# One block of a hybrid transformer on one core: the joint down stage with two block sums made by adding loads, an eighth pair by seven products, and pairs interleaved

## The chip, the cores and the metric

The kernel runs on one core of a Trainium2 chip. The metric is the time of one execution on the device, in microseconds (us); of several runs the median is taken. A core has TensorE (PE; its weight loads are listed as PEld), VectorE (DVE), ScalarE (ACT), GpSimd (POOL), SyncE (SP) and 16 DMA engines. Here SP issues the weight loads and POOL a second stream of loads.

## The reference

One transformer block over 256 tokens of width 2048: adaptive normalisation, one wide projection, a gated recurrence (HGRN2) in both directions, windowed attention with rotary positions, a gated merge, and a convolutional feed-forward network. The part that the change touches is the last product:

```python
def conv_ffn(h, w_up, conv_w, conv_b, w_down):
    a, u = jnp.split(h @ w_up, 2, axis=-1)
    return (jax.nn.silu(depthwise_conv(a, conv_w, conv_b)) * u) @ w_down
...
new_x = x_mid + mod_x[:, 5][:, None, :] * ffn_x
```

`w_down` is 5632 x 2048, that is 44 row blocks of 128. Everything is float32.

## The kernel before

Work runs as one stream of weights. A float32 product is made of three products of TensorE (`mm3`): both operands are split into a high part (float32r, a cast on ACT) and a low part (the rest, a subtraction on DVE), and high x high, high x low and low x high are added in PSUM. So each 512 KB of weights costs a load by SP into a buffer `raw`, a cast into `whi` on ACT and a subtraction into `wlo` on DVE, and PE reads both. There are four buffers `raw`, three `whi` and three `wlo`: a new block's cast waits until PE is done with the block three before it.

The feed-forward network is worked off in three groups of 16, 16 and 12 row blocks. `up(0)` and `up(1)` make the activations `g0` and `g1` of the first 32 row blocks; then the joint down stage (`down_two`) multiplies all 32 with `w_down`; then the third group follows. The joint stage has two halves of 1024 output columns each (`half`). Within a half the 32 row blocks are 16 pairs; a pair of row blocks, two groups of 128 tokens and two halves of 512 columns make a product of 2 x 2 by 2 x 2 blocks. Of a pair's weights, W11 and W12 are the two column halves of its first row block, W21 and W22 those of its second. A plain pair takes eight block products, that is 24 instructions on PE. The pairs in `SEVEN` take seven block products (Winograd's form of Strassen's scheme), 21 instructions: three go into `sev`, and four banks `norm` collect the rest. The seven products need four sums of weight blocks, T1 to T4, each split into high and low parts as well: `two` (L990) makes T1 (W11 and W12) and T3 (W12 and W22) in a tile `araw` with two additions of 128x512 on DVE (L991, L992; the signs are in the activations), `four` (L997) makes the other two from it (L998, L999). They need sums of activations too, which `seven_acts` makes in `up(0)` and `up(1)` for each pair in `SEVEN`.

`chunk` (L137) issues a block's load, cast and subtraction with a priority that is up to `LEAD` = 60 steps ahead, so that a scheduler puts them ahead of the products that stand before them in the program. Each engine then runs its queue strictly in that order; a waiting instruction holds all behind it. In the profile L143 is the cast in `chunk` and L144 the subtraction, L148 the load, L69 every product. L112 to L114 are the same three in the other stages. At the end of a half the seven-product banks are combined on DVE and ACT (L1005 to L1013), and `turn` transposes the result on PE (L1022) and adds it to the residual `xm` (L1025). The second half takes over the PSUM banks of the first.

## Time and profile before

| | |
|---|---|
| median of 3 runs | 1676.38 us (1675.18 to 1677.02) |
| profiled execution | 1675.59 us, of which 1673.8 us are the span from the first to the last instruction |
| joint down stage | from about 1296 to 1469 us of the span |
| PE busy | 1660.3 us, 99% of the span |
| DVE busy | 1264.6 us, 76% |
| ACT busy | 862.1 us, 52% |
| granted TensorE clock | 1.0 in every stretch |

The page lists busy times of engines, groups of equal instructions by source line, DMA queues, and the chain of waits that ended last. Starts and durations of single instructions are read from the timeline. A product of 128x512 shows a duration of 0.39 us, but the next one starts after about 0.23 us, since products are pipelined: PE's pace is read from starts, and a wait is a start that comes later than that.

### The profile page before, as it was taken

What the parts mean: (1) busy time and instruction counts of PE and PEld (TensorE: products, weight loads), DVE (VectorE), ACT (ScalarE), POOL (GpSimd) and SP (SyncE); (2) the same over time, 40 slices, a digit from 0 to 9 for tenths busy, and PEclk for the clock granted to TensorE, in tenths of its full rate; (3) what the DMA queues carried; (4) which work ended last, traced back from release to release, by engine and by line L of the source; (5) the groups of instructions that cost most, each with busy time, mean ns of one, the idle gap of its engine ahead of it and who ended that gap; (6) DMA issues with size and microseconds to landing.
All of it is one profiled execution on the core that took longest, in us unless ns stands there. A gap on an engine that the chain in (4) does not pass through costs nothing.

```text
span 1673.8 us, 25069 instructions
## 1 busy us (share of the span) xinstructions
PE 1660.3 (99%) x9508; PEld 1392.2 (83%) x9508; DVE 1264.6 (76%) x2014; ACT 862.1 (52%) x1323; POOL 68.3 (4%) x132
## 2 busy tenths in 40 slices
PE   8999999999999999999999999999999999999999
PEld 3668888888888888888888988888888777788887
DVE  3448985666879886878879887788767888866665
ACT  4337542433646764554455665555555555545542
POOL 0000100000000000001100000000000000000000
PEclk9999999999999999999999999999999999999999
DMA  9997834534466657878856577677555565655554
GB/s 378 408 356 246 286 122 158 178 111 154 162 216 211 214 202 277 285 242 280 285 202 234 182 247 256 212 273 252 191 183 190 185 212 187 201 183 192 187 199 149
DMA packets 104153, 371.85 MB, mean 222 GB/s; under 512 B 11488, under 2 KB 13920, under 8 KB 104032
## 3 DMA queue, kind: packets, MB, share of 16 engines
q1 hardware_dynamic: 85600, 303.14, 51.3%
q0 software_dynamic: 18432, 67.12, 12.3%
q8 instruction: 74, 1.21, 0.3%
q14 instruction: 47, 0.39, 0.1%
HBM read 368.11 MB, written 2.10 MB: 221 GB/s over the span
## 4 chain that ended last, share of the span: by engine, by line
PE 96%; DMA 2%; DVE 1%; ACT 0%; issue 0%; SPq 0%; DVEq 0%; ACTq 0%
PE bankm L69 85%; PE banks L69 9%; DMA ringv<-in_wst_dram 1%; DMA ringq<-in_wst_dram 1%; PE banks L406 0%; PE banks L610 0%; PE banks L779 0%; PE banks L602 0%; DVE wlo L114 0%; DMA xraw<-in_xct_dram 0%; PE banks L611 0%; PE banks L224 0%; PE banks L632 0%; PE banks L749 0%; PE banks L1022 0%
## 5 line engine op out<-in xcount | busy, mean ns | idle before, releaser
L69 PE MATMUL bankm<-hl,whi 128*128 128x512 f32 (+1 forms) x3136 | 970.4, 392 | 0.0
L114 DVE TENSOR_TENSOR wlo<-raw,whi 128x1024 fp32r<-128x1024 f32 (+2 forms) x434 | 528.1, 1218 | 240.0 <-ACT whi L113 238.2
L113 ACT CAST whi<-raw 128x1024 fp32r<-128x1024 f32 (+2 forms) x434 | 453.2, 1045 | 479.5 <-PE bankm L69 366.4
L69 PEld LDWEIGHTS bankm<-hl,wlo 128*128 128x128 f32 x2848 | 533.2, 188 | 120.6 <-DVE wlo L114 0.4
L69 PE MATMUL bankm<-hl,wlo 128*128 128x256 f32 (+2 forms) x2848 | 610.2, 287 | 0.0
L69 PEld LDWEIGHTS bankm<-hl,whi 128*128 128x128 f32 x3136 | 494.9, 189 | 20.3 <-DVE hl L153 0.4
L69 PE MATMUL bankm<-whi,hl 128*128 128x512 f32 x640 | 209.2, 395 | 1.2 <-ACT hl L245 1.0
L398 DVE SCALAR_TENSOR_TENSOR acc<-araw,csil,acc 128x1024 f32<-128x1024 f32 x120 | 153.4, 1279 | 2.1 <-DMA araw<-in_ada_dram 1.6
L69 PEld LDWEIGHTS bankm<-whi,hl 128*128 128x128 f32 x640 | 119.7, 188 | 28.0 <-ACT hl L245 2.6
L69 PE MATMUL bankm<-wlo,hl 128*128 128x512 f32 x320 | 124.7, 392 | 0.0
L393 POOL DMA_DIRECT2D araw<-in_ada_dram x128 | 68.1, 532 | 1092.2 <-DVE acc L398 566.9
L143 ACT CAST whi<-raw 128x1024 fp32r<-128x1024 f32 x64 | 61.1, 956 | 42.1 <-PE bankm L69 25.4
L69 PE MATMUL bankm<-yb,whi 128*128 128x512 f32 x256 | 80.7, 397 | 0.0
L144 DVE TENSOR_TENSOR wlo<-raw,whi 128x1024 fp32r<-128x1024 f32 x64 | 69.3, 1104 | 2.2 <-ACT whi L143 1.1
L69 PEld LDWEIGHTS bankm<-wlo,hl 128*128 128x128 f32 x320 | 60.1, 188 | 12.9 <-DVE wlo L144 0.4
L69 PEld LDWEIGHTS bankm<-yb,wlo 128*128 128x128 f32 x256 | 48.1, 188 | 11.3
L910 ACT ACTIVATE fs<-fs,prm 128x256 f32<-128x256 f32 x44 | 26.4, 601 | 49.8 <-DVE fs L464 49.8
L69 PE MATMUL bankm<-yb,wlo 128*128 128x256 f32 x256 | 50.6, 279 | 0.0
L143 ACT CAST whi<-araw 128x1024 fp32r<-128x1024 f32 x28 | 29.5, 1054 | 34.3 <-PE banks L69 17.0
L144 DVE TENSOR_TENSOR wlo<-araw,whi 128x1024 fp32r<-128x1024 f32 x28 | 34.3, 1224 | 16.2 <-ACT whi L143 14.5
L69 PE MATMUL bankm<-whi,g 128*128 128x512 f32 x136 | 46.1, 390 | 0.0
L226 DVE TENSOR_REDUCE tn<-banks 128x8 f32<-128x32 f32 (+1 forms) x9 | 1.7, 188 | 53.1 <-ACT whi L113 50.1
(281 smaller groups left out, 1538.9 us busy)
## 6 DMA issues: line engine op xcount, KB each, us to landing
raw<-in_wst_dram SPq DMA_DIRECT2D x489, 512.0 KB, 4.1
araw<-in_ada_dram POOLq DMA_DIRECT2D x128, 512.0 KB, 4.7
ringv<-in_wst_dram SPq DMA_DIRECT2D x24, 512.0 KB, 9.9
ringq<-in_wst_dram SPq DMA_DIRECT2D x20, 512.0 KB, 9.9
araw<-in_wst_dram SPq DMA_DIRECT2D x10, 512.0 KB, 9.9
xraw<-in_xct_dram SPq DMA_DIRECT2D x8, 512.0 KB, 7.3
raw<-in_wst_dram SPq DMA_DIRECT2D x7, 384.0 KB, 9.9
ringkT<-in_wst_dram SPq DMA_DIRECT2D x5, 512.0 KB, 9.9
```

What stands on the lines that cost most here:

```text
L69: return PE.matmul(o, l, r, start=start, stop=stop, skip_group_check=True)
L113: S.copy(hi, raw)
L114: self.last = V.tensor_tensor(lo, raw, hi.bitcast(F32), op=ALU.subtract)
L143: S.copy(hi[:, w], raw[:, w])
L144: V.tensor_tensor(lo[:, w], raw[:, w], hi[:, w].bitcast(F32), op=ALU.subtract)
L226: V.tensor_reduce(m8, aps[:, 0:w].rearrange("p (q g c) -> p q c g", q=2 * n, g=4)[:, :, 0:2, :], axis=AX.X, op=ALU.add)
L393: nc.gpsimd.dma_start(raw, ada2[idx])
L398: V.scalar_tensor_tensor(acc, raw, csil[:, kt, 0:1], acc, op0=ALU.mult, op1=ALU.add)
L910: S.activation(t, s, AF.Identity, bias=cb[:, f:f + 1], scale=cw[:, f, 1:2])
```

## The change

In the joint down stage:

- T1 and T3 of a pair of `SEVEN` are no longer made on DVE. `ahead` loads the pair's first row block into `araw` by SP, and then a load by POOL adds W12 and W22 (in rows of 512 elements) to the tile's two halves while it writes (`accum_op=ALU.add`). This second load waits for the first. It is placed up to 2 x `LEAD` steps ahead.
- W11 is loaded a second time, alone (256 KB), and its high and low parts have a tile of their own (`w1`, in the place `kT`, one buffer) instead of a `whi` and a `wlo`. `four`'s sums go to `t24`, in the place `acc`, one buffer.
- Pair 15 joins `SEVEN`; pair 14 is the last plain pair and closes the sums. Pairs 1 to 12 are interleaved: between the parts of a seven-product pair stand the two halves of the next plain pair. Pairs 13 and 15 follow without one.
- `turn` of the first half stands after one of the two blocks of pair 0 instead of after both; the combination of the banks comes after pair 15.
- POOL's scratch for descriptors is 4096 instead of 8192.

```diff
-SEVEN = (1, 3, 5, 7, 9, 11, 13)
+SEVEN = (1, 3, 5, 7, 9, 11, 13, 15)
...
-    def chunk(parts, make, tag="raw"):
+    def chunk(parts, make, raw=None):
         with tc.high_priority(offset=min(LEAD, max(0, tc.tile_snap_priority() - base[0]))):
-            raw = strm.tile([P, 1024], F32, name=tag, bufs=4 if tag == "raw" else 2)
-            hi, lo = [strm.tile([P, 1024], F32R, name=nm, bufs=3) for nm in ("whi", "wlo")]
-            make(raw)
+            if raw is None:
+                raw = strm.tile([P, 1024], F32, name="raw", bufs=4)
+            elif raw is big:
+                raw = big.tile([P, 1024], F32, name="t24", tag="acc")
             w = slice(0, 512 * parts)
+            if parts == 2:
+                hi, lo = [strm.tile([P, 1024], F32R, name=nm, bufs=3) for nm in ("whi", "wlo")]
+            else:
+                one = big.tile([P, 2, 512], F32R, name="w1", tag="kT")
+                hi, lo = one[:, 0, :], one[:, 1, :]
+            if make:
+                make(raw)
...
+        def ahead(p):
+            with tc.high_priority(offset=min(2 * LEAD, max(0, tc.tile_snap_priority() - base[0]))):
+                r = strm.tile([P, 1024], F32, name="araw", bufs=2)
+                nc.sync.dma_start(r, wst[at(p, 0)])
+                nc.gpsimd.dma_start(r.rearrange("p (k c) -> p k c", k=2),
+                                    wst[at(p, 0):at(p, 0) + 2, :, 512:].rearrange("k p c -> p k c"), accum_op=ALU.add)
+            return r
+
+        def normal(p, k, start=False):
+            a = acts(p)[2 * k:2 * k + 2]
+            _, ws = chunk(2, block(p, k))
+            for b, (x, w) in zip((0, 2, 1, 3), ((x, w) for w in ws for x in a)):
+                add(norm[b], x, w, start)
+
+        def seven(p, between=lambda k: None):
+            r2 = ahead(p)
...
+            rb, (w21, w22) = chunk(2, block(p, 1))
             add(norm[0], a12, w21)
             add(norm[1], s4, w22)
-            ra, (w11,) = chunk(1, fetch)
+            between(1)
+            _, (w11,) = chunk(1, block(p, 0, 512))
             add(sev[0], a11, w11, f, l)
-
-            def two(raw):
-                V.tensor_tensor(raw[:, 0:512], ra[:, 0:512], ra[:, 512:], op=ALU.add)
-                V.tensor_tensor(raw[:, 512:], ra[:, 512:], rb[:, 512:], op=ALU.add)
-            r2, (t1, t3) = chunk(2, two, "araw")
+            _, (t1, t3) = chunk(2, None, r2)
             add(sev[1], s1, t1, f, l)
             add(sev[3], a21, t3, f, l)
+            between(0)
...
-            r4, (t2, t4) = chunk(2, four, "araw")
+            _, (t2, t4) = chunk(2, four, big)
...
+        normal(0, 1, True)
+        before()
+        normal(0, 0)
+        for p in range(1, 13, 2):
+            seven(p, lambda k: normal(p + 1, k))
+        seven(13)
+        seven(15)
...
-    nc = bacc.Bacc("TRN2", target_bir_lowering=False, num_devices=1, dynamic_dma_scratch_size=8192)
+    nc = bacc.Bacc("TRN2", target_bir_lowering=False, num_devices=1, dynamic_dma_scratch_size=4096)
```

What the scheduler makes of it. First DVE's queue in the middle of the first half, over one seven-product pair and one plain pair, before (`raw_12428` is the pair's W21 and W22, `raw_12440` its W11 and W12, `araw_12449` holds T1 and T3, `araw_12462` T2 and T4, the last two rows are the plain pair):

```order
L144 TENSOR_TENSOR wlo_12430<-raw_12428,whi_12429 128x1024
L991 TENSOR_TENSOR araw_12449<-raw_12440 128x512
L992 TENSOR_TENSOR araw_12449<-raw_12440,raw_12428 128x512
L144 TENSOR_TENSOR wlo_12442<-raw_12440,whi_12441 128x512
L998 TENSOR_TENSOR araw_12462<-araw_12449,raw_12428 128x512
L999 TENSOR_TENSOR araw_12462<-araw_12462,raw_12428 128x512
L144 TENSOR_TENSOR wlo_12451<-araw_12449,whi_12450 128x1024
L144 TENSOR_TENSOR wlo_12464<-araw_12462,whi_12463 128x1024
L144 TENSOR_TENSOR wlo_12477<-raw_12475,whi_12476 128x1024
L144 TENSOR_TENSOR wlo_12495<-raw_12493,whi_12494 128x1024
```

And after (`w1_12630` is W11, `araw_12596` T1 and T3, `raw_12599` W21 and W22, `t24_12665` T2 and T4, `raw_12611` and `raw_12647` the plain pair):

```order
L152 TENSOR_TENSOR w1_12630<-raw_12629,w1_12630 128x512
L1001 TENSOR_TENSOR t24_12665<-araw_12596,raw_12599 128x512
L152 TENSOR_TENSOR wlo_12601<-raw_12599,whi_12600 128x1024
L1002 TENSOR_TENSOR t24_12665<-t24_12665,raw_12599 128x512
L152 TENSOR_TENSOR wlo_12613<-raw_12611,whi_12612 128x1024
L152 TENSOR_TENSOR wlo_12638<-araw_12596,whi_12637 128x1024
L152 TENSOR_TENSOR wlo_12649<-raw_12647,whi_12648 128x1024
L152 TENSOR_TENSOR wlo_12667<-t24_12665,whi_12666 128x1024
```

The two additions L991 and L992 are gone, and the first addition that reads the added tile (L1001) stands ahead of the subtraction of W21 and W22.

Second, DVE's queue at the end of the first half. Before, pair 13 (`raw_12677`, `raw_12689`) is followed by the plain pairs 14 and 15 and the first combinations of banks:

```order
L998 TENSOR_TENSOR araw_12711<-araw_12698,raw_12677 128x512
L999 TENSOR_TENSOR araw_12711<-araw_12711,raw_12677 128x512
L144 TENSOR_TENSOR wlo_12700<-araw_12698,whi_12699 128x1024
L144 TENSOR_TENSOR wlo_12713<-araw_12711,whi_12712 128x1024
L144 TENSOR_TENSOR wlo_12731<-raw_12729,whi_12730 128x1024
L1006 TENSOR_TENSOR yva_12142<-banks_12139,ykT_12141 128x512
L144 TENSOR_TENSOR wlo_12749<-raw_12747,whi_12748 128x1024
L144 TENSOR_TENSOR wlo_12767<-raw_12765,whi_12766 128x1024
```

After, from pair 13's T1 and T3 (`araw_12678`) through pair 15 (`araw_12724`) to pair 14 (`raw_12777`, `raw_12783`) and the next half's first block (`raw_12825`):

```order
L152 TENSOR_TENSOR wlo_12702<-araw_12678,whi_12701 128x1024
L152 TENSOR_TENSOR wlo_12713<-t24_12711,whi_12712 128x1024
L1001 TENSOR_TENSOR t24_12757<-araw_12724,raw_12727 128x512
L152 TENSOR_TENSOR wlo_12729<-raw_12727,whi_12728 128x1024
L152 TENSOR_TENSOR w1_12740<-raw_12739,w1_12740 128x512
L152 TENSOR_TENSOR wlo_12748<-araw_12724,whi_12747 128x1024
L1002 TENSOR_TENSOR t24_12757<-t24_12757,raw_12727 128x512
L152 TENSOR_TENSOR wlo_12759<-t24_12757,whi_12758 128x1024
L152 TENSOR_TENSOR wlo_12779<-raw_12777,whi_12778 128x1024
L152 TENSOR_TENSOR wlo_12785<-raw_12783,whi_12784 128x1024
L152 TENSOR_TENSOR wlo_12827<-raw_12825,whi_12826 128x1024
```

Two seven-product pairs now stand without a plain pair between them, and pair 15's L1001 stands ahead of three subtractions of that pair.

Third, SP's queue at the same place. Before, four loads of 512 KB to each two pairs:

```order
L148 DMA raw_12677<-in_wst_dram 128x1024
L148 DMA raw_12689<-in_wst_dram 128x1024
L148 DMA raw_12729<-in_wst_dram 128x1024
L148 DMA raw_12747<-in_wst_dram 128x1024
L148 DMA raw_12765<-in_wst_dram 128x1024
```

After (L972 is the load that POOL's adding load then waits for):

```order
L972 DMA araw_12678<-in_wst_dram 128x1024
L964 DMA raw_12647<-in_wst_dram 128x1024
L964 DMA raw_12681<-in_wst_dram 128x1024
L964 DMA raw_12693<-in_wst_dram 128x512
L964 DMA raw_12727<-in_wst_dram 128x1024
L972 DMA araw_12724<-in_wst_dram 128x1024
L964 DMA raw_12739<-in_wst_dram 128x512
```

A seven-product pair has three loads on SP instead of two, besides the adding load on POOL, and there are two buffers `araw`.

More of the change, by code (lines that the diff above doesn't have):

```diff
@@ L145, in chunk @@
         return raw, [(hi[:, 512 * i:512 * i + 512], lo[:, 512 * i:512 * i + 512]) for i in range(parts)]
-    def fetch(raw):
-        nc.sync.dma_start(raw, wst[st.half])
-        st.half += 1
     def split(hi, lo, src):
@@ L931, in seven_acts @@
             sums["a"] = big.tile([P, 5, 2, 3 * P], F32R, name="sa", tag="v")
-            sums["b"] = big.tile([P, 2, 2, 3 * P], F32R, name="sb", tag="sb")
+            sums["b"] = big.tile([P, 3, 2, 3 * P], F32R, name="sb", tag="sb")
         n = SEVEN.index(p)
@@ new lines, in acts, with block, at @@
+        def acts(p):
+            return act(2 * p, 0), act(2 * p, 1), act(2 * p + 1, 0), act(2 * p + 1, 1)
+        def block(p, k, c=1024):
+            return lambda raw: nc.sync.dma_start(raw[:, 0:c], wst[at(p, k), :, 0:c])
+        def at(p, k):
+            return st.half + 32 * n + 2 * p + k
+        def ahead(p):
[5 more added lines that the diff above has]
+            return r
@@ L1028, in down_two @@
     def down_two(g0, g1):
-        ys = lambda: [big.tile([P, 2, 512], F32, name="y" + t, tag=t) for t in ("kT", "va")]
         sev = [bank()]
@@ L1036, in down_two @@
         sev = [bank() for _ in range(4)]
-        y1 = []
-        half(1, g0, g1, norm, sev, y1, lambda: (turn(0, y0, sev), y1.extend(ys())))
+        half(1, g0, g1, norm, sev, y1, lambda: turn(0, y0, sev))
         turn(1, y1, None)
+        st.half += 64
     def down(g, gt, last):
```

54 lines of the change are left out of this document (18 added, 36 removed).

## The prediction

> **What bounds the kernel now.** I read the page first, then the joint down stage by stretches, its waits, and the timelines of PE, ACT and DVE in it.
>
> ```profile
> span 1673.8 us, 25069 instructions
> PE 1660.3 (99%) x9508; PEld 1392.2 (83%) x9508; DVE 1264.6 (76%) x2014; ACT 862.1 (52%) x1323; POOL 68.3 (4%) x132
> PE 96%; DMA 2%; DVE 1%; ACT 0%; issue 0%; SPq 0%; DVEq 0%; ACTq 0%
> ```
>
> PE is the chain that ended last (96%). So a change is worth the products it takes from PE plus the waits of PE that it ends, less those it makes. Now the stage (columns: stretch, length, PE, PEld, DVE, ACT, POOL busy, clock, DMA share, GB/s), one plain and one seven-product pair long:
>
> ```profile
> 1306.40:1316.90 10.50, 10.50 (x47) 8.36 (x46) 9.16 (x12) 5.79 (x6) 0.00 (x0) 1.00 0.62 200
> ```
>
> DVE is busy for 9.16 of 10.50 us, close behind PE. The clock is full. PE's pace and its one wait, from PE's timeline of such a stretch:
>
> ```profile
> 1339.07 0.62 PE L69 MATMUL bankm<-whi,g 128*128 128x512 f32 x2
> ...
> 1343.17 0.62 PE L69 MATMUL bankm<-whi,g 128*128 128x512 f32 x2
> ...
> 1345.67 0.39 PE L69 MATMUL banks<-whi,g 128*128 128x512 f32 x1
> 1346.01 0.50 PE L69 MATMUL banks<-wlo,sa 128*128 128x512 f32 x1
> 1346.35 0.40 PE L69 MATMUL banks<-whi,sa 128*128 128x512 f32 x1
> ```
>
> Between the first two rows lie 18 products: 4.10 / 18 = 0.228 us each. The last three rows are 0.34 us apart instead: 0.22 us lost where T1 and T3 (`sa`) come in. The waits of the stage (1280 to 1480) say how often:
>
> ```profile
> PEld banks L69 <- DVE wlo L144: 2.6, 7, 0.4
> PEld bankm L69 <- DVE wlo L144: 2.6, 7, 0.4
> ```
>
> Seven in each half, one for each seven-product pair: 14 x 0.22 = 3.1 us. Their cause, on ACT and DVE:
>
> ```profile
> 1343.64 1.05 ACT L143 CAST whi<-araw 128x1024 fp32r<-128x1024 f32 x1 [2.14 <-PE bankm L69]
> ```
> ```profile
> 1340.93 0.69 DVE L992 TENSOR_TENSOR araw<-raw 128x512 f32<-128x512 f32 x1
> 1341.54 0.69 DVE L144 TENSOR_TENSOR wlo<-raw,whi 128x512 fp32r<-128x512 f32 x1
> 1342.15 0.69 DVE L998 TENSOR_TENSOR araw<-araw,raw 128x512 f32<-128x512 f32 x1
> 1342.87 0.69 DVE L999 TENSOR_TENSOR araw<-araw,raw 128x512 f32<-128x512 f32 x1
> 1344.73 2.59 DVE L144 TENSOR_TENSOR wlo<-araw,whi 128x1024 fp32r<-128x1024 f32 x2 [1.17 <-ACT whi L143]
> ```
>
> The sums are ready at 1343.56, but the cast waits for a buffer: PE's last product from the block three before starts at 1343.17, the cast at 1343.64 (0.47 later), the subtraction at 1344.73, the low part is used at 1346.01. Such a turn of a buffer takes 2.84 us from last product to first use; 12 dense products (2.74 us) lie between. W11's half block stands in that rotation and is only three products long, which makes the cover short. The other wait is at the boundary of the halves:
>
> ```profile
> 1390.30 0.70 PE L69 MATMUL bankm<-whi,sa 128*128 128x512 f32 x2
> 1390.84 0.39 PE L69 MATMUL banks<-whi,hl 128*128 128x512 f32 x1
> 1391.46 0.50 PE L69 MATMUL bankm<-whi,hl 128*128 128x512 f32 x1 [0.23 <-ACT whi L143]
> 1391.79 0.39 PE L69 MATMUL banks<-whi,hl 128*128 128x512 f32 x1
> ```
>
> 1391.79 - 1390.30 = 1.49 us for four products, 0.58 too long. In all 3.1 + 0.6 = 3.7 us.
>
> **The change, part by part.**
>
> *Products.* Pair 15 takes 21 instead of 24 in each half: 6 x 0.228 = 1.37 us less, on the path. Its extra sums of activations on DVE in `up(1)` cost nothing: the subtractions there stand idle for ACT, which waits for PE,
>
> ```profile
> 1283.01 1.23 DVE L114 TENSOR_TENSOR wlo<-raw,whi 128x1024 fp32r<-128x1024 f32 x1 [1.23 <-ACT whi L113]
> 1285.85 1.23 DVE L114 TENSOR_TENSOR wlo<-raw,whi 128x1024 fp32r<-128x1024 f32 x1 [1.61 <-ACT whi L113]
> ```
>
> and they are first needed half a stage later.
>
> *W11 out of the rotation.* The tightest turn is then that of the plain pair's first block: it waits for the previous plain block, and between lie T2 and T4 (6 products), W21 and W22 (6) and its own first: 14 starts = 3.19 us against 2.84. It holds, so the 3.1 us go, in pairs 1 to 12. Were the pace of DVE in the way, they would stay: the ends are 0 and 3.1. But L991 and L992 (685 ns, below) leave DVE, 9.16 - 1.37 = 7.79 us of a stretch of 45 x 0.228 = 10.26. I take 3.1. `w1` and `t24` with one buffer each turn over once in 10.26 us and cost nothing: `w1`'s products end 4.8 us after a pair's start, the next `w1` is read at 14.4. At the start of the stage `w1` takes the place `kT` from `up(1)`,
>
> ```profile
> 1301.68 0.42 DVE L915 TENSOR_TENSOR fs<-fs,fs 128x256 f32<-128x256 f32 x1
> ```
> ```profile
> 1295.89 0.40 PE L69 MATMUL bankm<-whi,hl 128*128 128x512 f32 x1
> ```
>
> which is done with it at 1302.1; PE, from 1295.9, wants `w1` 42 products on, at 1305.5: 3.4 us for a cast of 0.6 and a subtraction of 0.7.
>
> *The boundary.* With `turn` earlier, PE still has 12 products (2.7 us) of pair 0 behind the last of the old half, and of DVE's last combinations (128x512, 0.61 each at the pace of the rows above) three are left by then: 1.8 us. I take the 0.6 as gone; ends 0 and 0.6.
>
> *The ends of the halves.* Here pairs 13 and 15 stand together. DVE per pair: three subtractions of 128x1024, one of 128x512 and two additions.
>
> ```profile
> L144 DVE TENSOR_TENSOR wlo<-raw,whi 128x1024 fp32r<-128x1024 f32 x50 | 59.8, 1220 | 2.1 <-ACT whi L143 1.1
> L991 DVE TENSOR_TENSOR araw<-raw 128x512 f32<-128x512 f32 x14 | 9.6, 685 | 1.1 <-DMA raw<-in_wst_dram 1.1
> L998 DVE TENSOR_TENSOR araw<-araw,raw 128x512 f32<-128x512 f32 x14 | 9.6, 686 | 0.0
> ```
> ```profile
> 1347.24 2.35 DVE L144 TENSOR_TENSOR wlo<-raw,whi 128x1024 fp32r<-128x1024 f32 x2
> ```
>
> Back to back they follow at 2.35 - 1.22 = 1.13 us, the small ones at 0.61 (1340.93, 1341.54, 1342.15). 3 x 1.13 + 3 x 0.61 = 5.2 us against PE's 21 x 0.228 = 4.79: DVE is the slower. With t = 0 at pair 13's first product: the buffer for its T2 and T4 comes free with pair 11's last product at -0.23, its cast runs from 0.24 to 1.29, its subtraction from 1.33. Behind it DVE's queue holds L1001 of pair 15 (2.47), then W21 and W22 (3.08), W11 (4.22), T1 and T3 (4.83), L1002 (5.97); ACT's cast of T2 and T4 runs from 6.70 to 7.75, DVE's subtraction ends at 9.01. PE, dense, wants it at 8.67: 0.4 us late with the latency. Then ACT's casts in a row (pair 14's two blocks, a copy, the next stage's first block, whose buffer is T2 and T4's) reach PE's queue, which has that block's first product after four of pair 14, another 0.4 late. 0.8 us per half, 1.7 in all; ends 0 (some cast found free earlier) and 3.1 (by full durations of 1.22 and 0.69 in place of the back-to-back pace).
>
> *The adding loads.* No row shows one. What is near:
>
> ```profile
> raw<-in_wst_dram SPq DMA_DIRECT2D x60, 512.0 KB, 4.1
> ```
> ```profile
> araw<-in_ada_dram POOLq DMA_DIRECT2D x128, 512.0 KB, 4.7
> ringv<-in_wst_dram SPq DMA_DIRECT2D x24, 512.0 KB, 9.9
> GB/s 378 408 356 246 286 122 158 178 111 154 162 216 211 214 202 277 285 242 280 285 202 234 182 247 256 212 273 252 191 183 190 185 212 187 201 183 192 187 199 149
> L393 POOL DMA_DIRECT2D araw<-in_ada_dram x128 | 68.1, 532 | 1092.2 <-DVE acc L398 566.9
> ```
> ```profile
> DMA to landing us min/median/max: 3.7/4.4/6.3
> ```
> ```profile
> DMA to landing us min/median/max: 3.0/4.1/5.2
> ```
>
> A load by SP lands after 4.1 us in this stage, one by POOL after 4.4 (the last row but one, 1000 to 1200 us; the last is `raw` again) to 4.7, and 9.9 where many were queued. An adding load must also read the tile: 0.52 MB more, at the 408 GB/s of the second slice 1.3 us. I take 4.6 + 6.5 = 11.1 us for plain and adding load: 4.1 and 4.7, the 1.3, and 1.0 for more load on the engines and twice as many rows. Ends: 3.0 (the shortest plain one) + 3.7 = 6.7, and 2 x 9.9 = 19.8.
>
> Time at hand: a buffer `araw` is free after the subtraction of T1 and T3 two pairs before. In the middle that is 2.55 after a pair's start (by the turn of a buffer as above: cast from 0.24, subtraction from 1.33), and L1001 two such pairs on comes 2.4 us ahead of its pair's start: 20.52 - 2.4 - 2.55 = 15.6 us. It fits. At the end it does not: pair 11's T1 and T3 are done at 2.55 - 10.26 = -7.7, and pair 15's L1001 is due at 2.47, since no plain pair lies between 13 and 15: 10.1 us. 11.1 is 1.0 late, and L1001 heads an unbroken row on DVE (three subtractions and L1002), so all of it reaches PE: 2 x 1.0 = 2.0 us. Behind L1001 on DVE is everything that PE is about to read; SP has only later loads behind the plain load, POOL nothing. Half 1's first L1001 has 11 us or more after its plain load is issued and then stands before combinations whose banks PE needs later: nothing.
>
> [...]
>
> *Other.* SP's five loads in place of four: each is a third of a us of issue in a stretch of 10 us. Half the scratch: POOL waits for buffers in the row above (released by DVE's `acc`), not for room; 0.
>
> **Sum**, on the profiled execution (1675.59; 1673.8 span and 1.8 around): -1.37 - 3.7 + 1.7 + 2.0 = -1.4: 1674.2. The median of the runs is 0.8 above that execution, so 1675.0.
>
> **Rivals.**
>
> *In time.* The two loads need 10.1 us or less. Then the 2.0 go: 1673.0, and 1671.3 if the ends of the halves hold too. For it: 4.1 + 4.7 is 8.8. Against it: the second reading of the tile, and half as much again on the engines.
>
> *Late.* The adding load is slow by itself. Each us over 10.1 costs two: from 4.4 us over (14.5 us in all) the kernel is slower than 1679.7. At 14.5 to 16 it ends at 1680 to 1683. For it: 9.9 us in the trace under load, twice in a row. Against it: the stage isn't that loaded now (0.62).
>
> *The DMA engines become the bound.* Four loads are 0.62 x 10.5 = 6.5 us of all engines in a stretch; after it there are 4.5 plain ones, 7.3, and the adding load. Counted as two, 3.3: 10.6 against 10.26, 0.3 a stretch, some 4 us over 12 stretches, on top of late ends: about 1684. If it counts as four: 13.8, over 1700. Against it: share is not rate; at 408 GB/s 4.5 loads take 5.8 us. [...]
>
> *No difference from interleaving*, that is the 0.22 stays somewhere else in each pair: about 1678, within the bound.
>
> **How the numbers follow.** Forecast (1 us late, small gain) 0.40, of which nearly all is within 0.2% (3.35 us, about what a measurement of this kernel can tell from no change: 1673.0 to 1679.7). In time 0.28, some two thirds of it below 1673.0 (0.19), and the forecast's own spread adds 0.05: 0.24. No difference 0.06. Late 0.16 and engines full 0.10, nearly all slower: 0.26. Same is the rest, 0.50. The range goes from 1671.8 (in time, and half of the ends' cost) to 1683 (late by 5), which leaves out the lowest few and most of the full engines; the forecast's own is 1673 to 1678.
>
> **What would show it.** PE's starts 0.228 us apart where T1 and T3 come in, with no wait there in pairs 1 to 12; DVE about 7.8 us busy in 10.3; one wait of PE for DVE near each half's end, of 1 to 2 us, with DVE's L1001 of pair 15 waiting for the adding load. The landing time of the adding loads decides: under 6 us the rival "in time", over 10 the late one; a DMA share near 1 with growing landing times of `raw` the last. The prediction is wrong if PE waits inside pairs 1 to 12, or if the ends of the halves show no wait at all.

## The result, and the profile after

| | before | after |
|---|---|---|
| median | 1675.78 us (4 runs) | 1690.64 us (1689.45 to 1694.47, 4 runs) |
| ratio | | 1.0092, 95% interval 1.0074 to 1.011 |
| span of the profiled execution | 1673.8 us | 1692.7 us |

The kernel is 0.9% slower, outside the range of 1671.8 to 1683.0. The profiled execution of after took 1694.5 us, 3.8 above its median; what follows explains the spans' 18.9 us. The page of after:

```profile
span 1692.7 us, 25166 instructions
...
PE 1663.7 (98%) x9502; PEld 1395.3 (82%) x9502; DVE 1253.3 (74%) x2000; ACT 865.4 (51%) x1329; POOL 87.5 (5%) x148
...
PE 85%; DMA 8%; issue 3%; DVE 3%; ACT 1%; SPq 0%; POOL 0%; DVEq 0%; ACTq 0%; POOLq 0%
```

PE made up 96% of the chain before, now 85%; loads have 8%. DVE has 11 us less to do, as the change meant, and it brought nothing. The waits of the stage (1290 to 1490; us in total, times, longest):

```profile
ACT w L151 <- DMA raw<-in_wst_dram: 18.7, 11, 3.9
PEld bankm L69 <- DVE wlo L152: 18.5, 14, 6.3
...
PE bankm L69 <- DVE wlo L152: 12.8, 5, 5.9
DVE t L1001 <- DMA araw<-in_wst_dram: 12.8, 2, 6.6
```

DVE waited twice for an adding load, once at each half's end. The chain of waits at the second one (start, us, what):

```profile
1454.19 6.37 DMA araw<-in_wst_dram
...
1461.18 9.32 DMA araw<-in_wst_dram
...
1470.59 0.10 DVE t L1001
...
1471.20 1.23 DVE wlo L152
...
1472.47 1.22 PE bankm L69 x2
```

Pair 15's plain load takes 6.4 us and its adding load 9.3, 16.3 us from the first issue to the landing; L1001 and the subtraction behind it follow, and PE. PE's timeline there:

```profile
1466.63 0.39 PE L69 MATMUL bankm<-whi,g 128*128 128x512 f32 x1
1472.47 0.79 PE L69 MATMUL bankm<-wlo,g 128*128 128x512 f32 x1 [5.45 <-DVE wlo L152]
1473.06 0.63 PE L69 MATMUL bankm<-whi,g 128*128 128x512 f32 x1
1473.49 0.63 PE L69 MATMUL banks<-whi,sb 128*128 128x512 f32 x1
1473.92 0.63 PE L69 MATMUL banks<-wlo,sb 128*128 128x512 f32 x1
```

PE starts 5.84 us after its last product, and then every 0.43 us instead of 0.228, until 1478.6. The stage by stretches shows why (columns as before; the clock is the third number from the end):

```profile
1306.40:1316.90 10.50, 10.50 (x48) 8.70 (x47) 10.24 (x15) 6.61 (x8) 1.17 (x1) 1.00 0.75 213
1348.40:1358.90 10.50, 10.21 (x44) 8.12 (x45) 7.00 (x8) 5.48 (x6) 1.17 (x1) 1.00 0.88 268
1369.40:1380.00 10.60, 4.71 (x20) 3.60 (x19) 3.88 (x5) 2.71 (x4) 1.18 (x1) 0.82 0.62 139
1470.00:1481.00 11.00, 8.53 (x24) 6.40 (x24) 7.59 (x8) 5.18 (x6) 0.00 (x0) 0.69 0.43 143
```

The granted clock, here a mean over the row, falls to 0.82 and 0.69 where the long waits are; in the trace's own record of the clock it is 0.5 for 6.8 us behind each of them. DVE is relieved (7.0 us in the second row), and the DMA share is 0.75 to 0.88 where it was 0.62.

To add up the loss I summed how much later than 0.228 us each product of PE starts after the one before it (starts over 0.3 us apart, 1285 to 1500 us). Before: 4.0 us. After: 23.1 us, of which the two long waits 11.7, the slow products behind them 4.8, waits inside the pairs 5.3 (3.9 in the first half, 1.4 in the second), the rest 1.4. With six products less: 23.1 - 4.0 - 1.4 = 17.8 of the spans' 18.9 us. "PE's lateness" below is this sum.

### The profile page after: what moved, and what is told of

Read it like the earlier page. It is cut to its first block, busy times and chain, and to the rows that moved or that the text cites. A ratio compares the mean times of both kernels' runs of the same rounds, so it can differ in the third digit from the quotient of the medians.

```text
span 1692.7 us, 25166 instructions
## 1 busy us (share of the span) xinstructions
PE 1663.7 (98%) x9502; PEld 1395.3 (82%) x9502; DVE 1253.3 (74%) x2000; ACT 865.4 (51%) x1329; POOL 87.5 (5%) x148
## 4 chain that ended last, share of the span: by engine, by line
PE 85%; DMA 8%; issue 3%; DVE 3%; ACT 1%; SPq 0%; POOL 0%; DVEq 0%; ACTq 0%; POOLq 0%
PE bankm L69 77%; PE banks L69 5%; DMA raw<-in_wst_dram 3%; DMA araw<-in_wst_dram 1%; DMA ringv<-in_wst_dram 1%; DVE wlo L152 1%; DMA ringq<-in_wst_dram 1%; DMA ringkT<-in_wst_dram 1%; DVE wlo L114 1%; PE banks L410 0%; PE banks L614 0%; PE banks L783 0%; DMA araw<-in_ada_dram 0%; PE banks L606 0%; DMA xraw<-in_xct_dram 0%
## 5 line engine op out<-in xcount | busy, mean ns | idle before, releaser
L69 PE MATMUL bankm<-whi,hl 128*128 128x512 f32 x624 | 203.7, 395 | 1.7 <-ACT hl L249 0.9
L152 DVE TENSOR_TENSOR wlo<-raw,whi 128x1024 fp32r<-128x1024 f32 x48 | 58.4, 1219 | 6.0 <-ACT whi L151 5.5
L151 ACT CAST whi<-raw 128x1024 fp32r<-128x1024 f32 x48 | 50.1, 1051 | 22.7 <-PE bankm L69 9.0
L69 PE MATMUL bankm<-whi,g 128*128 128x512 f32 x112 | 39.6, 400 | 0.0
L69 PEld LDWEIGHTS bankm<-yb,whi 128*128 128x128 f32 x256 | 39.0, 189 | 0.1
L915 DVE SCALAR_TENSOR_TENSOR fs<-fs,prm,fs 128x255 f32<-128x255 f32 x44 | 21.3, 483 | 23.4 <-ACT fs L914 23.4
```

The source lines that it names most:

```text
L69: return PE.matmul(o, l, r, start=start, stop=stop, skip_group_check=True)
L151: S.copy(hi[:, w], raw[:, w])
L152: V.tensor_tensor(lo[:, w], raw[:, w], hi[:, w].bitcast(F32), op=ALU.subtract)
L915: V.scalar_tensor_tensor(t[:, 1:T], s[:, 0:T - 1], cw[:, f, 0:1], t[:, 1:T], op0=ALU.mult, op1=ALU.add)
```

## The experiments

Ratios are to the kernel before, run beside each. The lateness is that of the profiled execution.

| kernel | median us | ratio, 95% interval | PE's lateness |
|---|---|---|---|
| plain_pool | 1676.88 | 1.0009 (0.9999 to 1.0019) | 6.4 |
| add_rows4k | 1693.22 | 1.0093 (1.0080 to 1.0107) | 23.2 |
| no_w11 | 1683.41 | 1.0052 (1.0037 to 1.0067) | 14.4 |
| dve15 | 1680.14 | 1.0032 (1.0019 to 1.0045) | 12.0 |
| seven7 | 1677.20 | 1.0009 (1.0000 to 1.0018) | 6.0 |
| araw3 | 1686.53 | 1.0063 (1.0046 to 1.0080) | 17.4 |
| add_even | 1688.61 | 1.0078 (1.0064 to 1.0091) | 19.6 |
| dve_all | 1684.80 | 1.0055 (1.0037 to 1.0073) | 15.2 |
| plain_spread | 1673.68 | 0.9986 (0.9977 to 0.9995) | 3.0 |
| w11_own | 1674.84 | 0.9995 (0.9987 to 1.0004) | 5.9 |
| w11_own8 | 1676.22 | 1.0000 (0.9991 to 1.0009) | 5.9 |
| before_w1 | 1677.50 | 1.0005 (0.9996 to 1.0014) | 5.1 |
| w1_raw5 | 1676.16 | 1.0005 (0.9996 to 1.0014) | 6.2 |
| spread8 | 1681.22 | 1.0029 (1.0018 to 1.0039) | 9.4 |
| pool_two | 1691.35 | 1.0096 (1.0082 to 1.0110) | 20.4 |
| waits_dose | 1726.14 (1 run) | | 52.8 |

### What an adding load costs

plain_pool, an edit to after:

```diff
-  wst[at(p, 0):at(p, 0) + 2, :, 512:].rearrange("k p c -> p k c"), accum_op=ALU.add)
+  wst[at(p, 0):at(p, 0) + 2, :, 512:].rearrange("k p c -> p k c"))
```

> The load by POOL keeps its place, its bytes from DRAM and its waits, but writes instead of adding; T1 and T3 are then not sums (the output is another). If adding itself is what makes the load slow (it reads the tile too: 7.5 us median landing in the kernel after, against 4.4 for the plain POOL loads before), it lands in about 4.7 us, the raw loads go back from 5.5 to about 4.5, the two long waits of 6.3 and 5.8 us shrink by some 3 us each and most of the slow products behind them go: about 1682 us. If its shape (256 rows of 2 KB) or the mere additional bytes do it, the landings stay at 7 us or so and the time at 1690.

add_rows4k, another:

```diff
-  nc.gpsimd.dma_start(r.rearrange("p (k c) -> p k c", k=2),
-      wst[at(p, 0):at(p, 0) + 2, :, 512:].rearrange("k p c -> p k c"), accum_op=ALU.add)
+  nc.gpsimd.dma_start(r, wst[at(p, 1)], accum_op=ALU.add)
```

> The adding load adds one whole row block, 128 rows of 4 KB, instead of two half blocks in 256 rows of 2 KB; bytes, place and waits are the same (T1 and T3 are other sums, so the output is another). With plain writing in its place the kernel takes 1676.9 us and its POOL loads land in 5.5 us, with the adding 7.3 us in this stage. Theory that the small rows (3808 packets of the POOL queue in this stage, against 2016 with plain writing) cost it: landings near 5.5 us, time 1676 to 1680. Rival, that adding costs by itself, per byte: landings stay at 7 us or more, the POOL queue's share of the engines near 25%, time over 1686.

Without the addition nearly all of the loss goes, more than expected, since the waits inside the pairs go too; with rows of 4 KB nothing changes. The DMA part of the stage (1300 to 1480; queue, packets, MB, share of 16 engines; then issues with the median landing), first of after:

```profile
q0 software_dynamic: 3808, 7.34, 25.8%
...
raw<-in_wst_dram SPq DMA_DIRECT2D x46, 512.0 KB, 5.0
araw<-in_wst_dram SPq DMA_DIRECT2D x14, 512.0 KB, 6.0
araw<-in_wst_dram POOLq DMA_DIRECT2D x14, 512.0 KB, 7.3
raw<-in_wst_dram SPq DMA_DIRECT2D x15, 256.0 KB, 5.9
```

of plain_pool:

```profile
q0 software_dynamic: 2016, 7.34, 12.9%
...
raw<-in_wst_dram SPq DMA_DIRECT2D x52, 512.0 KB, 4.5
araw<-in_wst_dram SPq DMA_DIRECT2D x14, 512.0 KB, 4.9
araw<-in_wst_dram POOLq DMA_DIRECT2D x14, 512.0 KB, 5.5
raw<-in_wst_dram SPq DMA_DIRECT2D x15, 256.0 KB, 4.6
```

and of add_rows4k:

```profile
q0 software_dynamic: 2016, 7.34, 24.7%
...
araw<-in_wst_dram POOLq DMA_DIRECT2D x14, 512.0 KB, 7.6
```

Q0 is POOL's queue. Its 14 loads hold all 16 engines for 0.258 x 180 / 14 = 3.3 us each when they add, with rows of either size (3.2), and 1.7 us when they write (1.8 in plain_spread below). So here an adding load costs the engines two plain ones (25.8% against 12.9%), and the other loads of after land later than plain_pool's (W11's after 5.9 instead of 4.6 us). Why the addition doubles the time, no run shows.

### The long waits at the ends

dve15 is after, where pair 15 alone takes T1 and T3 from DVE:

```diff
...
-            r2 = ahead(p)
+            add_load = p != 15
+            r2 = ahead(p) if add_load else None
...
-            _, (w11,) = chunk(1, block(p, 0, 512))
+            ra, (w11,) = chunk(1, block(p, 0, 512 if add_load else 1024))
...
+            def two(raw):
+                V.tensor_tensor(raw[:, 0:512], ra[:, 0:512], ra[:, 512:], op=ALU.add)
+                V.tensor_tensor(raw[:, 512:], ra[:, 512:], rb[:, 512:], op=ALU.add)
-            _, (t1, t3) = chunk(2, None, r2)
+            r2, (t1, t3) = chunk(2, None, r2) if add_load else chunk(2, two, strm)
```

> Pair 15 alone makes T1 and T3 on DVE again (two additions of 128x512, from one load of W11 and W12 by SP); pairs 1 to 13 keep their adding loads. Theory that pair 15's two loads one after the other cost the two long waits, and these the slow products behind them: 12.1 + about 4.5 us go, some 1.4 us of DVE work at each half's end comes, doubled by what stands behind it: about 1677 (1675 to 1680). Rival, that the adding loads slow the whole stage through the DMA engines: the long waits turn up elsewhere, over 1684.

No start there is over 0.77 us late, and no slow products follow. 1680.1 is at the upper edge of what the first theory expected: of the 12.0 us of lateness 5.8 are the waits inside the pairs, which stayed, and some 6 are shorter ones at the ends and just behind them, where the theory allowed 2.8. seven7 keeps all adding loads and undoes the eighth pair:

```diff
-SEVEN = (1, 3, 5, 7, 9, 11, 13, 15)
+SEVEN = (1, 3, 5, 7, 9, 11, 13)
...
-        for p in range(1, 13, 2):
+        for p in range(1, 15, 2):
             seven(p, lambda k: normal(p + 1, k))
-        seven(13)
-        seven(15)
...
-        n11, n21, n12, n22 = acts(14)
+        n11, n21, n12, n22 = acts(15)
...
```

> The kernel after without its eighth pair: pair 15 is plain again and closes the sums, pair 14 is interleaved with pair 13, so that no two seven-product pairs adjoin; adding loads and W11's separate load stay. Theory that the long waits come from pair 15's two loads having 10 us at hand where they need 16 to 17: with 15.6 us everywhere the two long waits (11.7 us) and the slow products behind them (5 us) go, 1.4 us come for six more products: about 1677 us (1675 to 1680), with the waits inside the pairs as before, 4 to 6 us. Rival, that two loads of 16 to 17 us are too long for 15.6 as well, as the 17.9 us in add_even were: waits of 2 us and more in the last pairs, over 1682.

1677.2 us: the first theory to the number. Adding loads of 7.6 us (median) do no harm here, where a pair has 15.6 us everywhere; the long waits came from pair 15's place behind pair 13. araw3 gives the time in another way:

```diff
-                r = strm.tile([P, 1024], F32, name="araw", bufs=2)
+                if SEVEN.index(p) % 3 == 2:
+                    r = big.tile([P, 1024], F32, name="araw", tag="va")
+                else:
+                    r = strm.tile([P, 1024], F32, name="araw", bufs=2)
```

> Three tiles for the sums T1 and T3 instead of two (every third pair uses a place that is free until a half ends), so that pair 15's plain and adding load have one pair more, about 20 us in place of 10. Adding loads and everything else stay. Theory that the long waits at the ends (6.3 and 5.8 us, and the slow products behind them) come from too little time for two loads in a row: they go, the waits inside pairs 1 to 12 stay; about 1679 us (1677 to 1682), near the 1680.1 that pair 15's sums on DVE gave. Rival, that the adding loads saturate the engines so that any earlier load makes another late: over 1685.

The long waits at the ends went, and the kernel gained only some 5 us (each by its own runs of the kernel before): others came early in each half, of up to 3.4 us. Its chain there:

```profile
1313.60 10.40 DMA araw<-in_wst_dram
...
1324.08 0.69 DVE t L1004
...
1325.96 4.21 PE bankm L69 x9
```

With three tiles a third pair of loads is issued early, and an adding load that a pair needs now takes 10.4 us. The rival had part of it: loads issued earlier make others late. add_even halves the adding loads (dve15's edit with another condition):

```diff
-            add_load = p != 15
+            add_load = SEVEN.index(p) % 2 == 0
```

> The kernel after, with adding loads for pairs 1, 5, 9 and 13 only; pairs 3, 7, 11 and 15 make T1 and T3 on DVE from one load of W11 and W12. Theory that the loss is the engines' time for adding loads and their lateness: half of them, each with a plain load's time more, and no separate W11 load in the other pairs: waits inside pairs 1 to 12 fall from about 5 us to 2 or less, ends as in dve15 (about 2 us each): 1677 to 1679. Rival, that the interleaved order with one tile t24 binds by itself (dve_all: 1684.8): over 1682.

Both expectations missed the cause: the adding loads were later, not earlier (chain of waits):

```profile
1336.97 10.01 DMA araw<-in_wst_dram
...
1347.05 0.69 DVE t L1008
...
1348.94 1.33 PE bankm L69 x3
```

The plain load ahead of it was issued at 1329.03, so the two took 17.9 us where some 15.6 are at hand; PE waited 3.35 us. The median landing of the seven adding loads in the stage is 8.9 us, though the stage's share is 0.69 instead of 0.80. In the 10 us of this one the share is 0.92: the loads of SP come in a burst beside it. What sets a single adding load between 5.6 and 10.6 us beyond that isn't settled.

### The waits inside the pairs

no_w11, an edit to after:

```diff
-            _, (w11,) = chunk(1, block(p, 0, 512))
+            _, (w11,) = chunk(1, None, rb)
```

> W11 is not loaded by itself; its high and low parts are made from the block of W21 and W22 that is there anyway (the output is another). Theory that W11's separate load, which stands in SP's queue and in the four raw buffers, makes the waits inside pairs 1 to 12 (about 5 us in all): they go, and with 256 KB less per pair the landings drop a little, which shortens the long waits by about 1 us each: about 1684 us, DMA share in the middle from 0.85 to about 0.75. Rival, that the adding loads alone keep the DMA engines busy: middle waits stay, over 1688.

The waits inside the pairs are gone (in each half no start over 0.1 us late until pair 13), with adding loads as slow as before (7.1 us). The time is the expected one, though the long waits shrank otherwise than expected: 5.7 us are left in the first half (6.0 in after), and 1.5 and 2.2 in the second (5.6). plain_pool kept W11's load, and there they are gone but for 0.7 us. So they take both: W11's separate load and engines kept busy by adding loads. How, shows in seven7's chain, where they recur in each pair:

```profile
1421.14 1.15 DVE wlo L152
1422.30 5.74 DMA raw<-in_wst_dram
...
1428.11 0.63 ACT w L151
...
1431.80 1.15 DVE wlo L152
```

A subtraction on DVE frees a buffer `raw`, W11's load goes into it, and ACT's cast of W11 waits, at the head of ACT's queue. The buffers have no more loads than before: SP's trace has 64 loads into `raw` in the stage of before and of after, four to each two pairs; the fifth load of SP goes into `araw`, so the count of five in the expectation below is wrong. What binds is a loop. W11's subtraction, L1001, L1002 and two other subtractions follow one another on DVE, the last of them frees the buffer for the next pair's W11, and so one turn holds W11's load, its cast and this row on DVE: 10.66 us from the first row to the last, where PE needs 10.26. With the 4.6 us that W11's load takes in plain_pool the turn would be about 9.5 (an estimate from these rows), which fits. w11_own takes W11 out of them, in seven7:

```diff
+            elif raw is cons:
+                raw = big.tile([P, 1024], F32, name="w11", tag="va")
...
-            _, (w11,) = chunk(1, block(p, 0, 512))
+            _, (w11,) = chunk(1, block(p, 0, 512), None if f else cons)
```

> seven7 with W11's load in a place of its own (one that is free until a half ends; the first pair of a half keeps the buffer raw) instead of one of the four buffers raw. In seven7 the remaining waits (6.0 us, nearly all inside the pairs) have a chain of DVE's last reader of a buffer raw, W11's load of 5.6 to 6.3 us and its cast. Theory that the turn of the buffers raw, with five loads in them instead of four, makes W11 late: the waits go, 1672.5 to 1673.5 us, faster than the kernel before. Rival, that the DMA engines (share 0.80) make every load late: stays at 1677.

Against seven7, each by its own runs of the kernel before, that is 1.7 us (+1.2 to -0.5), with intervals that overlap; what is clear is that ACT's waits for W11 (18.4 us in seven7) are gone. But in the profiled execution PE now starts 1.7 us late in one pair of each half, behind this row of DVE's timeline (L1003 is after's L1001):

```profile
1362.74 0.69 DVE L1003 TENSOR_TENSOR t<-araw,raw 128x512 f32<-128x512 f32 x1 [3.03 <-issue]
```

DVE stood still for 3 us ahead of the addition that reads the adding load's tile and the block W21 and W22. The landings tell for which: W21 and W22 were there at 1353.17, while the adding load, issued at 1352.55, has this one:

```profile
DMA to landing us min/median/max: 10.1/10.1/10.1
```

It landed at 1362.66, just ahead of the row above. From the issue of the plain load ahead of it, at 1344.87, the two took 17.8 us, against the 15.6 at hand; in the second half they took 17.9, with an adding load of 11.1. So with W11 out of the way the adding loads are late in the middle of the halves too, once in each. In the second half fourteen of the load's sixteen completions had come after 7.5 us and the last after 11.1: its landing is that of the last one.

w11_own8 adds the eighth pair, with dve15's edit and pair 14's blocks around pair 15 (as in plain_spread below):

> w11_own with the eighth pair back: pair 15 by seven products with T1 and T3 made on DVE from one load, pair 14's two blocks on both sides of it. In plain_spread the ends so arranged cost 2.2 us of waits in one half and none in the other. Six products less are 1.4 us; DVE has 1.4 us more to do in each half's end: 1671.5 to 1674, equal to w11_own or 1 us better. Rival, that DVE's four additions in pair 15 are late as in dve15 (2 us at each end): 1675 or more.

w11_own8 comes out at the rival's time, but not for its reason: its two largest waits (2.3 and 0.9 us) are in the middle of the halves again, the first behind an adding load of 11.4 us. Neither kernel beats the one before by more than its interval. What was left of the new waits cost as much as the old ones.

### The parts without adding loads

before_w1 is one part of the change alone, in the kernel before:

```diff
-            hi, lo = [strm.tile([P, 1024], F32R, name=nm, bufs=3) for nm in ("whi", "wlo")]
+            if parts == 2:
+                hi, lo = [strm.tile([P, 1024], F32R, name=nm, bufs=3) for nm in ("whi", "wlo")]
+            else:
+                one = big.tile([P, 2, 512], F32R, name="w1", tag="acc")
+                hi, lo = one[:, 0, :], one[:, 1, :]
```

> The kernel before, with one edit: W11's high and low parts have a tile of their own (a place that is free in the stage) and take no buffer of the three whi and wlo. Prediction's step: the 14 waits of 0.22 us where T1 and T3 come in (3.1 us) go: 1672.7 us (1672 to 1673.5), ratio 0.998. Rival, that DVE with 9.2 of 10.5 us has no room to be earlier and the waits stay: 1675.6, no change.

No gain. Of the waits of 0.22 hardly any is left, but four of 0.5 to 1.2 us are there. Its chain (L1003 is the last addition of T2 and T4, L147 the cast):

```profile
1409.33 0.70 DVE araw L1003
...
1410.09 4.42 DMA raw<-in_wst_dram
...
1414.58 0.63 ACT w L147
```

The next turn of a buffer, that of `raw`, is as tight as the one that was relieved. w1_raw5 gives it a fifth buffer (and halves POOL's scratch for the room):

```diff
...
-            raw = strm.tile([P, 1024], F32, name=tag, bufs=4 if tag == "raw" else 2)
+            raw = strm.tile([P, 1024], F32, name=tag, bufs=5 if tag == "raw" else 2)
...
```

> before_w1 with a fifth buffer raw in the whole kernel (POOL's scratch for descriptors is halved for the room). In before_w1 the old waits are gone, but four new ones of 0.5 to 1.2 us stand in their place, and their chain runs from T2's and T4's last addition, which frees a buffer raw, through a load of 4.4 us to W11's cast. Theory that the four buffers raw are the next to bind: with five the new waits go too: 1672.7 us (1672 to 1674). Rival, that DVE itself (9.2 of 10.5 us) is too late for W11's parts: no change from 1677.5.

Still no gain: a few single waits are there (2.1, 1.0 and 0.8 us in the profiled execution). The first stands behind a load that was slow once, 6.9 us; the second behind DVE's additions of `turn` (L1029); the third wasn't taken apart. The time is the rival's, no change, but DVE too late for W11's parts isn't what the trace has. spread8, before_w1 with pair 15 in `SEVEN` and pair 14's blocks on both sides of it:

> before_w1, and pair 15 by seven products, all sums on DVE; pair 14's two blocks stand on both sides of pair 15, so that no two seven-product pairs adjoin, and the second one closes the sums. Gain of 6 products, 1.4 us, below before_w1 if DVE holds: pairs 13 and 15 with pair 14 need 15.1 us of DVE against 15.1 of PE, so a wait of up to 1 us at each half's end: 1671.3 to 1673.5. Rival, that DVE's own combinations of the banks come in between and cost more than the six products: over 1675.

The rival's side: 1681.2, with waits up to 1.6 us at the ends. Which of DVE's additions decides there wasn't taken apart. dve_all is dve15's edit with `add_load = False`, all sums on DVE:

> No adding loads at all: every seven-product pair makes T1 and T3 on DVE from one load of W11 and W12; the tile of W11's parts, the eighth pair and the interleaving stay. Theory that all of the loss is the adding loads and W11's separate load: no wait inside pairs 1 to 12 (DVE 9.2 of 10.3 us a stretch still fits), -1.4 for the products, -3.7 for the old waits, and ends of the halves worse than with adding loads would have been, since pairs 13 and 15 need 13.2 us of DVE against 9.6 of PE: +2 to +3.5 per half. 1675.8 - 5.1 + 4 to 7 = 1675 to 1678. Rival, that the eighth pair and the interleaving do harm of their own: over 1680.

1684.8, on the rival's side. The first row of its waits:

```profile
ACT whi L153 <- DVE t L1009: 26.9, 11, 4.3
```

ACT, whose queue holds every later cast behind it, waits for DVE's last addition of T2 and T4: with all sums on it DVE is late in the interleaved order. pool_two puts T1 and T3 on GpSimd, in w1_raw5:

```diff
-                V.tensor_tensor(raw[:, 0:512], ra[:, 0:512], ra[:, 512:], op=ALU.add)
-                V.tensor_tensor(raw[:, 512:], ra[:, 512:], rb[:, 512:], op=ALU.add)
+                nc.gpsimd.tensor_tensor(raw[:, 0:512], ra[:, 0:512], ra[:, 512:], op=ALU.add)
+                nc.gpsimd.tensor_tensor(raw[:, 512:], ra[:, 512:], rb[:, 512:], op=ALU.add)
```

> w1_raw5, with the two additions of T1 and T3 on GpSimd (a third way to take them from DVE). If GpSimd adds 128x512 in under 1.5 us and doesn't slow DVE, DVE has 7.8 of 10.3 us and no wait stays: 1672 to 1673, as w1_raw5 or better. Rival, that GpSimd needs 2 us or more for one, or that DVE's instructions get longer beside it: waits of 1 us and more in each pair, over 1685.

1691.4 us, the rival's side:

```profile
L995 POOL TENSOR_TENSOR araw<-raw 128x512 f32<-128x512 f32 x14 | 23.1, 1647 | 255.2 <-DMA raw<-in_wst_dram 237.0 <-DVE wlo L148 18.3
...
L1002 DVE TENSOR_TENSOR araw<-araw,raw 128x512 f32<-128x512 f32 x14 | 20.6, 1470 | 9.1 <-POOL araw L995 8.9
```

GpSimd takes 1.6 us for an addition, and DVE's first addition of T2 and T4, which runs in the same time, 1470 ns instead of 683 in w1_raw5.

plain_spread shows what the change's frame is worth if the sums cost only a plain load, and no two seven-product pairs adjoin (plain_pool with):

```diff
         seven(13)
+        normal(14, 1)
         seven(15)
...
-        for b, u1, u2, v1, v2 in ((0, n11, n12, w11, w21), (1, n11, n12, w12, w22), (2, n21, n22, w11, w21),
-                                  (3, n21, n22, w12, w22)):
-            add(norm[b], u1, v1)
-            add(norm[b], u2, v2, stop=True)
+        for b, u, v in ((0, n11, w11), (1, n11, w12), (2, n21, w11), (3, n21, w12)):
+            add(norm[b], u, v, stop=True)
```

> plain_pool (POOL's load writes and doesn't add; the output is another) with pair 14's two blocks on both sides of pair 15. Tells what the change would give if the sums cost a plain load and no two seven-product pairs adjoined. Theory that the rest of the loss in plain_pool, some 5 us of waits in the last pairs of the halves, is DVE falling behind in two adjoining pairs: with 2.7 us of products between them most of it goes: 1672 to 1674. Rival, that the combinations of the banks at the end cost it: stays at 1676 or more.

1673.7 us, a gain of 0.14% (0.05 to 0.23%), and 3.5 us better than plain_pool, each by its own runs of the kernel before: most of the ends' waits came from adjoining pairs. What is left stands in the first half's last pairs (0.5 us, behind POOL's load, which lands 1.0 us after DVE asks for it) and at the start of the second half (1.9 us), where DVE and then PE have these rows:

```profile
1376.46 0.69 DVE L1001 TENSOR_TENSOR t<-araw,raw 128x512 f32<-128x512 f32 x1 [1.89 <-DMA raw<-in_wst_dram]
1381.27 0.50 PE L69 MATMUL banks<-whi,hl 128*128 128x512 f32 x1 [0.91 <-DVE ykT L1019]
```

The second half's first L1001 waits for W21 and W22, and the combinations of the banks that PE needs stand behind it on DVE.

### The slow products

waits_dose makes PE wait for DVE alone, in the kernel before, with no load that is late:

```diff
-                V.tensor_tensor(raw[:, 512:], raw[:, 0:512], rb[:, 0:512], op=ALU.add)
+                for _ in range(1 + {(0, 3): 4, (0, 7): 8, (0, 11): 12, (1, 3): 6, (1, 7): 10, (1, 11): 16}.get((n, p), 0)):
+                    V.tensor_tensor(raw[:, 512:], raw[:, 0:512], rb[:, 0:512], op=ALU.add)
```

> The kernel before, with the last addition of T2 and T4 repeated in pairs 3, 7 and 11 (4, 8 and 12 times more in the first half, 6, 10 and 16 in the second; the result is the same), which makes PE wait for DVE and for no load. At 0.61 us each and some 1.3 us of room in a stretch the waits are about 1.1, 3.6 and 6.0, and 2.4, 4.8 and 8.5 us, 26 us in all. Theory that a long wait alone makes the granted clock fall, so that products follow at 0.43 instead of 0.23 us for some 10 products: slow products stand behind the waits of 5 us and more and not behind those of about 1 us, and the sum is over the waits by some 2 us for each: about 1708. Rival, that the slow products need the full DMA engines beside them: none here, and 1702.

```profile
1319.00:1323.80 4.80, 4.58 (x13) 3.30 (x13) 4.21 (x5) 2.70 (x3) 0.00 (x0) 0.64 0.56 201
1346.50:1351.30 4.80, 4.72 (x11) 3.30 (x12) 4.78 (x6) 2.93 (x3) 0.00 (x0) 0.54 0.57 189
1351.30:1356.00 4.70, 4.70 (x23) 3.85 (x22) 3.04 (x4) 0.65 (x2) 0.00 (x0) 1.00 0.67 218
```

The first two rows begin at the end of waits of 1.45 and 4.35 us, the third follows the second. With a DMA share of 0.57 the clock falls behind each wait (to 0.54 as a mean over the second row) and is back 4 to 6 us later. So the slow products are a cost of waiting itself: 2 to 3 us on top of a long wait. Against the expectation they follow the wait of 1.45 us too. The waits came out longer than expected (33 us in all), hence 1726 instead of 1708.

## Why the prediction was wrong, point by point

- **The adding loads** (+2.0) are the step that failed, by size. The sum of 11.1 us was built from a plain load of 4.6 and an adding load of 6.5; the trace has 6.4 to 7 and 9.1 to 9.3, 16.3 us and more. The 1.3 us for reading the tile, which an addition needs, were an estimate from its bytes; no run shows the reading by itself, only that an adding load holds the engines for 3.3 us and a plain one for 1.7. The mechanism stood: pair 15's L1001 late, all of it reaching PE, both halves. "Each us over 10.1 costs two" stood as well: 6 us over gave 11.7. The rival "late" had this, but the prediction gave it its small chance because "the stage isn't that loaded now": it took the load of before, though the next rival counted what the change adds. That rival's own times were too low by some 2 us, for they leave out the 1.7 of the ends: by the forecast's terms 14.5 to 16 us for the two loads give 1681.8 to 1684.8, and slower than 1679.7 starts at 13.5.
- **The DMA engines.** That rival said: an adding load counted as two is 3.3 us, 10.6 against 10.26 a stretch. It is 3.3 us (25.8% x 180 / 14). The prediction used it for a rate only; with engines at 0.75 to 0.88 the landing times had grown already (a plain load into `araw` lands after 6.0 us and an adding one after 7.3, both medians, where the weight loads of before landed after 4.1 at 0.62), and its own sum had only 1.0 us for the added load and the rows together.
- **After a long wait** it charged the wait alone. The clock's fall (4.8 us) stood in no term.
- **W11 out of the rotation** (-3.1): the step named the tightest turn of `whi` and `wlo` and stopped there. The waits of 0.22 went, as the first pairs of after and before_w1 show, but the turn of the four `raw` is next, with W11's load, now apart, in a loop of 10.7 us against PE's 10.26 (5.3 us inside the pairs of after: the sign that the prediction itself had named). "In the middle it fits" held for the adding loads in after and seven7, not in w11_own, and not for W11's load. With the adding taken out the gain would have stood: plain_pool's pairs lose 0.7 us.
- **The ends** (+1.7): plain_pool loses 3.2 us in the last pairs of its halves and 1.0 at the first block behind them. Of these 1.1 stand behind POOL's load, which is 1.0 us late for DVE even without the addition. So DVE does fall behind in two adjoining pairs, by about 3.2 us where 1.7 was booked.
- **The boundary** (-0.6): 0.5 us are still there behind each half of after, and 1.9 at the start of plain_spread's second half, where the next half's first L1001 holds up the combinations. The prediction had put that L1001 at nothing.
- **Products** (-1.4) and DVE's relief (7.0 us in the stretch shown) came as predicted.

## What to carry to other kernels

Price a load that adds by the time for which it holds the DMA engines (here that of two plain loads, 3.3 us against 1.7), and price its landing on the engines as the change leaves them (7.3 us here), not as the trace of before shows them (4.4 to 4.7 for plain loads by POOL). When a buffer is taken out of a tight rotation, follow the next one around before booking the gain: here `whi`, then `raw`, then the adding loads each bound at the same level. And when two producers need a fixed time one after the other, look for the one place where the pattern's spacing breaks (here two pairs side by side at the end); undoing that alone gave back nearly all of the loss.

## What the runs showed of the hardware

- A long wait of PE cost more than its length. Behind waits of 4 us and more the granted clock was 0.5 and products 0.43 us apart for 4 to 6 us. The slow pace also followed waits of 1.45 us (waits_dose), 1.89 (dve_all) and 2.1 (pool_two), while 2.17 (no_w11) and 2.1 (w1_raw5) had none behind them. The clock's own record in the traces tells these apart. In each of the 18 traces all changes of the clock in this stage lie on one grid of 3.41 us (the half clock of after lasts from 1376.20 to 1383.03 and from 1471.77 to 1478.60), as in these rows of waits_dose, cut at its steps:

```profile
1316.75:1320.16 3.41, 1.90 (x8) 0.95 (x7) 2.19 (x4) 2.45 (x3) 0.00 (x0) 1.00 0.41 135
1320.16:1323.58 3.42, 3.42 (x10) 2.65 (x9) 2.83 (x4) 1.54 (x2) 0.00 (x0) 0.50 0.44 147
1323.58:1326.99 3.41, 3.41 (x17) 2.78 (x16) 2.73 (x4) 0.62 (x1) 0.00 (x0) 1.00 0.58 179
```

Take as idle what passes between two starts of PE beyond 0.228 us, and add it up for every step between 1285 and 1500 us that ran at the full clock. The next step ran at half the clock after 18 of them, all with 2.06 us of idleness or more, and at the full clock after 1101, all with 2.03 or less. Two of the 18 are in after (3.02 and 3.41 us), where no other such step has over 1.50. So in these traces the idleness within a step tells the two apart, and the length of one wait does not: the wait of 1.45 us shares its step (2.06) with shorter ones, and w1_raw5's 2.1 us are split between two steps (1.33 and 0.88). This was read off the traces afterwards, and no run was made to test it; the two bounds lie close together.

- POOL was busy for 1.18 us to issue an adding load of 256 rows (after), 0.86 for one of 128 rows of 4 KB (add_rows4k), and 0.71 for plain_pool's, against 0.53 for the plain loads of before (L393).
